# Weight lo parts and one convolution tile of the second block: summed by adding DMA transfers instead of VectorE and GpSimd

## The chip, the cores and the metric

The kernel runs on one core of a Trainium2 chip. Its time is what the device takes for one launch, in microseconds (us); the times shown are the median and the extremes of three runs, and one more execution was recorded by the hardware profiler. The engines are TensorE (PE; its weight loads are PEld), VectorE (DVE), ScalarE (ACT), GpSimd (POOL) and SyncE (SP), which issues the ordinary DMA transfers. Each engine works through its own list of instructions in order.

## The reference, cut to what matters

Two transformer blocks follow each other on a sequence of 1024 tokens of width 1024, all in float32. The first has a Fourier mix, a latent attention, a cross attention to a memory and a mixture of 16 experts. The second is the one that the change touches:

```python
h = rmsnorm(x) * (1 + scale) + shift
proj = h @ w_in                       # 1024 x 10240
glu_a, glu_b, z_conv, q, k, v, z_att, g_conv, g_att = split(proj)
u = glu_a * sigmoid(glu_b)
u = depthwise_conv(u, conv_w, 31 taps, causal) + conv_b
y_conv = (silu(layernorm(u)) * silu(z_conv)) @ w_conv_out
y_att  = dilated window attention of q, k, v in three groups, times silu(z_att), @ w_att_out
x = x + gate * ((sigmoid(g_conv) * y_conv + sigmoid(g_att) * y_att) @ w_o)
```

## The kernel before, in words

**Split numbers.** TensorE multiplies in a short format (float32r), so every operand is split into a hi part (the value rounded to that format) and a lo part (value less hi), and a product is made of three matmuls: hi hi, hi lo, lo hi (`mm3`, `gemm_t`, lines 676 to 688). `split_to` (line 653) makes the hi part with a copy on ScalarE, and the lo part with a subtraction on VectorE or GpSimd; `ve()` (line 645) deals these calls out in a fixed ratio, in the second block one in four to GpSimd, at its end one in eight.

**Weight tiles.** `in2` (line 1597) makes one 128-channel tile of `proj`: it loads a 128 x 8 x 128 weight tile (512 KB) on SP, splits it (`wtile`, line 665) and runs 48 matmuls of 512 columns on it. There are 80 such tiles. In each group of three matmuls the last needs the lo part of the weights.

**Convolution.** `conv_tile` (line 1619) makes the gated input `u` of 128 channels, and then 31 taps of a shifted multiply and add into a page `o` (`conv`). Seven of the eight tiles do it on VectorE, one instruction for each tap. Tile 3 (`POOL_CONV`) does it in two: ScalarE multiplies a shifted `u` into a page `ct`, and GpSimd adds it to `o`. The taps are not issued at once: `tick` (line 690) takes one or two off a list after each half of a weight tile's matmuls, and ties them to these matmuls.

**Attention.** `att_pair` (line 1697) runs 12 times: q, k and v tiles by `in2`, the rotary positions on VectorE (`rope2`: `rt`, `rq`, `ro`), stacked copies on ScalarE (`qs`, `ks`), zeros on GpSimd (`kl`), ScalarE's copy of v (`vf`), its transposes on TensorE (`vt`), then scores, softmax and the product with v. Tiles of gates (`z_conv`, `z_att`, `g_att`, later `g_conv`) lie between as filling.

**Planner.** All operations of the program are recorded first, with a price and a latency, and `schedule` (line 283) orders them by a list rule: of the operations that are ready on an engine, the one recorded earliest. It lays buffers into 50 equal SBUF pages (`PAGES`, 4 KB on each of 128 partitions). An operation that needs a new page may start early only while the count of pages that all operations before it still need leaves one over; if not, it is held until earlier operations are done (`allowed`, line 310). What follows an operation waits for its end, which includes its latency, plus 0.5 us on another engine; on the same engine the latency is taken off again (line 378):

```python
lat = op.end + (self.LAT if o.eng != e else (0.07 if e == "dve" else 0.0) - op.lat)
```

The order that comes out is fixed in the program; at run time each engine keeps it and waits for the true ends. The profile puts nearly all instructions on one line, L180, the recording helper, so they are told apart by their tiles' names.

Of the kernel before, what the change touches and what calls it, by code (L numbers as in the profile page):

```python
# [8 lines left out]
F32 = mybir.dt.float32  # L9
F32R = mybir.dt.float32r  # L10
# [3 lines left out]
ACT = mybir.ActivationFunctionType  # L14
AX = mybir.AxisListType
P = 128
NT = 1024
# [171 lines left out]
class Program:  # L189
# [199 lines left out]
    def issue(self, order):  # L389
        with self.tc.manual_schedule():  # L390
            for op in order:
                for t in op.new:
                    pool, tag = self.pools[t.kind]
                    t.real = pool.tile(list(t.shape), t.dt, tag=f"{tag}{t.slot}", name=t.name)
                op.fn()
# [135 lines left out]
IN2 = {"glu_a": 0, "glu_b": 8, "z_conv": 16, "q": 24, "k": 36, "v": 48, "z_att": 60, "g_conv": 64, "g_att": 72}  # L531
# [47 lines left out]
class Kern(Program):  # L579
# [819 lines left out]
    def scatter_add(self, rows, idx, x):  # L1399
# [3 lines left out]
                in_=x.ap(), in_offset=None, compute_op=OP.add)  # L1403
        self.record("pool", 1.3, 4.0, issue, [x, idx], [rows]).dma = 1.46

    def tr8(self, x, base, n=8):

        h, l = self.page(base + "h", F32R, (P, 8, P)), self.page(base + "l", F32R, (P, 8, P))
        for c in range(0, n, 4):
            m = min(4, n - c)  # L1410
            ps = self.pb(base, (P, m, P))
            for k in range(m):
                self.pe.transpose(ps[:, k], x[:, (c + k) * P:(c + k + 1) * P], self.ident)
            self.split_to(h[:, c:c + m], l[:, c:c + m], ps, lo="dve")
        return h, l
# [180 lines left out]

    def in2(self, part, m, evac):
        n = len(self.ops)
        w = self.wtile(self.a["w_in2"][IN2[part] + m], 8, "w2")
        if self.in2_free:  # L1600
            self.in2_free -= 1
        else:
            self.ops[n].deps.add(self.x3_loaded)
        self.ops[n + 1].deps.add(self.moe_end)
        self.gemm_t(w, self.h2, evac, base=part, ticks=TICKS[part[0]])
# [13 lines left out]
    def conv_tile(self, i, cd):  # L1619

        u = self.in2_tanh("glu_b", i, "u")
        self.in2("glu_a", i, lambda c, ps: self.dve.scalar_tensor_tensor(u[:, c], u[:, c], 1.0, ps, OP.add, OP.mult))
        o = self.page("conv")
        w = lambda t: self.convw[:, i, t:t + 1]
        b = GV2["conv_b"] + i
        if i in POOL_CONV:
            back = self.back[1].append
            back(lambda: self.act.activation(o, u, ACT.Identity, scale=w(30), bias=self.gv2[:, b:b + 1]))

            def mul(t, n):  # L1630
                self.conv_tmp = self.page("ct")
                return self.act.activation(self.conv_tmp[:, :n], u[:, :n], ACT.Copy, scale=w(t))

            for t in range(29, -1, -1):
                s = 30 - t
                back(lambda t=t, s=s: mul(t, NT - s))
                back(lambda s=s: self.pool.tensor_tensor(o[:, s:], o[:, s:], self.conv_tmp[:, :NT - s], OP.add))
        else:
            back = self.back[0].append
            tap = self.dve.scalar_tensor_tensor  # L1640
            back(lambda: self.dve.tensor_scalar(o, u, w(30), self.gv2[:, b:b + 1], OP.mult, OP.add))
            for t in range(29, -1, -1):
                back(lambda t=t, s=30 - t: tap(o[:, s:], u[:, :NT - s], w(t), o[:, s:], OP.mult, OP.add))
        back(lambda: self.sp.dma_start(cd[i], o))
        back(lambda: self.conv_add(o))
# [383 lines left out]
```

## Time and profile before

| | us |
|---|---|
| median of 3 runs | 2770.51 (2767.68 to 2771.46) |
| the profiled execution, its own time | 2771.41 |
| its span, first to last instruction | 2769.3 |
| TensorE busy | 2659.9 |
| VectorE busy | 2096.2 |
| ScalarE busy | 1362.1 |
| GpSimd busy | 505.6 |

The span is what the traced instructions cover; busy time is the union of an engine's instructions in it. The second block's weight tiles begin at 1467 us and end at 2541 us. The granted clock is TensorE's: 1.00 is the upper of its two levels (2.4 GHz), 0.50 the lower (1.2 GHz).

### The profile page before, as it was taken

The page shows a single profiled execution, that of the slowest core. Times are in us where ns is not written, and L with a number is a line of the kernel's source. Part 1 is how long each engine was busy: PE and PEld are TensorE (multiplying, and loading weights), DVE is VectorE, ACT ScalarE, POOL GpSimd, SP SyncE. Part 2 cuts the span into 40 slices and gives each one's busy share as a digit, 9 for nine tenths or more (in the row PEclk, how much of TensorE's full clock was granted, in tenths as well). Part 3 has the DMA queues.
Part 4 walks back from the last instruction along what each step waited for, and adds up shares of the span by engine and source line. Part 5 has one row for each costly group of instructions (what it writes and reads, how often), then busy time and mean ns, then how long its engine had stood idle before and what let it go on. Part 6 is the DMA issues. An engine that isn't in the chain of part 4 may idle for free. (4 is left out here: it accounts for less than half of the span.)

```text
span 2769.3 us, 36068 instructions
## 1 busy us (share of the span) xinstructions
PE 2659.9 (96%) x13230; PEld 2232.0 (81%) x13230; DVE 2096.2 (76%) x3075; ACT 1362.1 (49%) x2177; POOL 505.6 (18%) x270
## 2 busy tenths in 40 slices
PE   8999999999994999999988998999999999999998
PEld 6888888888884888888867877788888888887887
DVE  7367876457567989988978789988889997649553
ACT  6156776333345877777774154534334434524221
POOL 1025555211004200101110133401100002002000
PEclk9999999999996999999999999999999999999999
DMA  4100112545347999999984011212212233449941
GB/s 174 34 34 9 39 54 92 175 154 180 124 139 283 342 358 359 357 356 387 380 302 172 16 61 61 77 54 90 78 42 73 77 137 138 152 164 309 340 173 53
DMA packets 130144, 457.06 MB, mean 165 GB/s; under 512 B 15299, under 2 KB 17539, under 8 KB 129969
## 3 DMA queue, kind: packets, MB, share of 16 engines
q1 hardware_dynamic: 125360, 438.00, 43.7%
q0 software_dynamic: 4608, 16.78, 2.4%
q8 instruction: 104, 1.70, 0.2%
q14 instruction: 72, 0.58, 0.1%
HBM read 378.73 MB, written 69.70 MB: 162 GB/s over the span
## 5 line engine op out<-in xcount | busy, mean ns | idle before, releaser
L180 DVE SCALAR_TENSOR_TENSOR conv<-u,convw,conv 128x1003 f32<-128x1003 f32 (+19 forms) x210 | 298.0, 1426 | 2.2
L180 DVE TENSOR_TENSOR w_upl<-w_up,w_uph 128x1024 fp32r<-128x1024 f32 x128 | 149.2, 1221 | 22.6 <-ACT w_uph L180 21.7
L180 DVE TENSOR_TENSOR w_downl<-w_down,w_downh 128x1024 fp32r<-128x1024 f32 x128 | 149.0, 1222 | 13.3 <-ACT w_downh L180 12.5
L180 DVE TENSOR_TENSOR w_gatel<-w_gate,w_gateh 128x1024 fp32r<-128x1024 f32 x123 | 144.0, 1220 | 7.5 <-ACT w_gateh L180 5.2
L180 ACT CAST w_gateh<-w_gate 128x1024 fp32r<-128x1024 f32 x128 | 125.7, 1057 | 5.7 <-issue 3.3
L180 ACT CAST w2h<-w 128x1024 fp32r<-128x1024 f32 x80 | 83.2, 1050 | 88.9 <-DMA w<-in_w_in_dram 62.1
L180 ACT CAST w_downh<-w_down 128x1024 fp32r<-128x1024 f32 x128 | 126.0, 1054 | 1.4 <-PE ea L180 1.4
L180 ACT CAST w_uph<-w_up 128x1024 fp32r<-128x1024 f32 x128 | 125.7, 1055 | 1.4 <-PE ea L180 0.7
L180 DVE TENSOR_TENSOR w2l<-w,w2h 128x1024 fp32r<-128x1024 f32 x64 | 87.2, 1364 | 37.7 <-ACT w2h L180 19.8
L180 POOL TENSOR_TENSOR wl<-w,wh 128x1024 fp32r<-128x1024 f32 (+3 forms) x31 | 57.3, 1849 | 310.6 <-ACT wh L180 253.3
L180 ACT CAST wh<-w 128x1024 fp32r<-128x1024 f32 (+3 forms) x71 | 62.5, 894 | 78.4 <-DMA w<-in_w_convout_dram 31.6
L180 ACT ACTIVATE ap<-ap,amx 128x128 f32<-128x128 f32 (+1 forms) x192 | 85.5, 449 | 25.5 <-DVE amx L180 25.2
L180 POOL TENSOR_TENSOR conv<-conv,ct 128x1023 f32<-128x1023 f32 (+29 forms) x30 | 74.8, 2493 | 115.5 <-ACT ct L180 115.1
L180 POOL TENSOR_TENSOR w2l<-w,w2h 128x1024 fp32r<-128x1024 f32 x16 | 43.8, 2734 | 263.2 <-ACT w2h L180 208.4
L180 DVE TENSOR_TENSOR ptl<-pt,pth 128x512 fp32r<-128x512 f32 x128 | 81.4, 684 | 8.7 <-ACT pth L180 6.7
L180 ACT ACTIVATE p<-p,mx 128x1024 f32<-128x1024 f32 x64 | 73.8, 1155 | 23.6 <-DVE mx L180 17.3
L180 POOL TENSOR_SCALAR p<-p,sum 128x1024 f32<-128x1024 f32 x64 | 74.2, 1166 | 59.0 <-DVE sum L180 52.7
L180 PE MATMUL eb<-w_uph,hth 128*128 128x512 f32 x256 | 80.5, 394 | 0.1
L1401 POOL DMA_INDIRECT x<-ey,idx x16 | 25.4, 1586 | 302.4 <-ACT ey L180 193.7
L180 PE MATMUL eb<-w_upl,hth 128*128 128x512 f32 x256 | 79.6, 392 | 0.7 <-DVE w_upl L180 0.5
L180 PE MATMUL ea<-w_gateh,hth 128*128 128x512 f32 x256 | 80.1, 393 | 0.0
L180 PE MATMUL ea<-w_gatel,hth 128*128 128x512 f32 x256 | 79.6, 392 | 0.4 <-DVE w_gatel L180 0.4
(554 smaller groups left out, 8663.1 us busy)
## 6 DMA issues: line engine op xcount, KB each, us to landing
w_gate<-in_w_gate_dram SPq DMA_DIRECT2D x128, 512.0 KB, 6.7
w_up<-in_w_up_dram SPq DMA_DIRECT2D x128, 512.0 KB, 6.9
w_down<-in_w_down_dram SPq DMA_DIRECT2D x128, 512.0 KB, 8.1
w<-in_w_in_dram SPq DMA_DIRECT2D x89, 512.0 KB, 4.1
wada<-in_w_adaT_dram SPq DMA_DIRECT2D x24, 512.0 KB, 6.4
convr<-cd SPq DMA_DIRECT2D x16, 512.0 KB, 6.2
amd<-sg SPq DMA_DIRECT2D x16, 512.0 KB, 5.7
ks<-ks SPq DMA_DIRECT2D x24, 256.0 KB, 2.9
```

The lines of the kernel that those rows point to most:

```text
L180: getattr(k.engines[eng], fn)(*[r(x) for x in a], **{n: r(x) for n, x in kw.items()})
L1401: self.nc.gpsimd.indirect_dma_start(out=rows.ap(), out_offset=bass.IndirectOffsetOnAxis(ap=idx.ap(), axis=0), in_=x.ap(), in_offset=None, ...
```

## The change

In `in2` the lo part is no longer a subtraction. ScalarE makes the hi part as before, and then a second copy, the negated hi part, into the lo part's page. A DMA transfer issued by GpSimd adds the raw weights to that page (`add_dma`, a new helper). In `conv_tile`, for tile 3, the addition of each tap to `o` is such a transfer as well, in place of GpSimd's tensor addition; ScalarE's multiplications stay. The planner is told a price of 1.1 us on GpSimd, a latency of 3.0 us, and the transfer's share of SP's queue.

```diff
+    def add_dma(self, out, x):
+
+        def issue():
+            self.nc.gpsimd.dma_start(out=out.ap(), in_=x.ap(), accum_op=OP.add)
+        op = self.record("pool", 1.1, 3.0, issue, [x, out], [out])
+        op.dma = 4 * int(np.prod(x.shape)) / 360e3
+        return op
...
     def in2(self, part, m, evac):
         n = len(self.ops)
-        w = self.wtile(self.a["w_in2"][IN2[part] + m], 8, "w2")
+        raw = self.load(self.a["w_in2"][IN2[part] + m], "w2", (P, 8, P), "wr")
+        w = [self.page("w2" + q, F32R, (P, 8, P)) for q in "hl"]
+        self.act.copy(w[0], raw)
+        self.act.activation(w[1], w[0].bitcast(F32), ACT.Copy, scale=-1.0)
+        self.add_dma(w[1].bitcast(F32), raw)
...
                 s = 30 - t
                 back(lambda t=t, s=s: mul(t, NT - s))
-                back(lambda s=s: self.pool.tensor_tensor(o[:, s:], o[:, s:], self.conv_tmp[:, :NT - s], OP.add))
+                back(lambda s=s: self.add_dma(o[:, s:], self.conv_tmp[:, :NT - s]))
```

## Rows read from the trace of the kernel before

**Rows 1.** The page, part 1: busy us, share of the span, instructions of TensorE.
```profile
PE 2659.9 (96%) x13230; PEld 2232.0 (81%) x13230; DVE 2096.2 (76%) x3075; ACT 1362.1 (49%) x2177; POOL 505.6 (18%) x270
```

**Rows 2.** Stretches: us; busy (count) of PE, PEld, DVE, ACT, POOL; clock; DMA; GB/s.
```profile
1445.00:1467.00 22.00, 8.41 (x44) 6.33 (x42) 11.21 (x22) 12.23 (x21) 3.19 (x2) 0.70 0.83 286
1467.00:2541.00 1074.00, 1042.66 (x5120) 875.10 (x5121) 899.15 (x1348) 427.54 (x869) 162.03 (x67) 0.98 0.29 99
1567.00:1800.00 233.00, 214.67 (x1039) 179.13 (x1038) 205.08 (x286) 112.02 (x214) 90.56 (x40) 0.96 0.18 59
2446.00:2541.00 95.00, 89.91 (x390) 74.00 (x388) 79.82 (x55) 29.69 (x42) 13.54 (x2) 0.96 0.74 235
```

**Rows 3.** Waits of TensorE, 1440 to 2560 us: total, times, longest.
```profile
PE vt L180 <- ACT vf L180: 13.4, 5, 7.2
```

**Rows 4.** Order of time on TensorE: start, length, instruction, idle before and releaser.
```profile
1671.11 1.76 PE L180 MATMUL vt<-ident,vf 128*128 128x128 f32 x7 [7.21 <-ACT vf L180]
...
1740.31 1.86 PE L180 MATMUL vt<-ident,vf 128*128 128x128 f32 x8 [3.49 <-ACT vf L180]
```

**Rows 5.** Stretches as in rows 2, around these two waits.
```profile
1668.80:1679.00 10.20, 7.09 (x31) 6.70 (x32) 8.08 (x25) 7.97 (x19) 0.00 (x0) 0.50 0.22 51
1740.40:1744.00 3.60, 3.60 (x15) 3.21 (x15) 3.57 (x2) 1.65 (x3) 3.16 (x2) 0.53 0.43 101
```

**Rows 6.** The page, part 5: groups of instructions; busy us, mean ns, idle before.
```profile
L180 ACT CAST w2h<-w 128x1024 fp32r<-128x1024 f32 x80 | 83.2, 1050 | 88.9 <-DMA w<-in_w_in_dram 62.1
...
L180 DVE TENSOR_TENSOR w2l<-w,w2h 128x1024 fp32r<-128x1024 f32 x64 | 87.2, 1364 | 37.7 <-ACT w2h L180 19.8
...
L180 POOL TENSOR_TENSOR conv<-conv,ct 128x1023 f32<-128x1023 f32 (+29 forms) x30 | 74.8, 2493 | 115.5 <-ACT ct L180 115.1
L180 POOL TENSOR_TENSOR w2l<-w,w2h 128x1024 fp32r<-128x1024 f32 x16 | 43.8, 2734 | 263.2 <-ACT w2h L180 208.4
```

**Rows 7.** Groups on VectorE, 1567 to 1800 us, columns as in rows 6.
```profile
L180 DVE SCALAR_TENSOR_TENSOR conv<-u,convw,conv 128x1002 f32<-128x1002 f32 (+29 forms) x44 | 82.2, 1868 | 0.5
L180 DVE TENSOR_TENSOR w2l<-w,w2h 128x1024 fp32r<-128x1024 f32 x12 | 19.4, 1614 | 6.0 <-DMA od<-of 2.2 <-DMA cd<-conv 1.9 <-PE apt L180 1.7
```

**Rows 8.** The same for 1800 to 2446 us.
```profile
L180 DVE SCALAR_TENSOR_TENSOR conv<-u,convw,conv 128x1019 f32<-128x1019 f32 (+21 forms) x146 | 190.0, 1311 | 1.3
```

**Rows 9.** Line 1401, the experts' adding scatter (512 KB): ns min/median/max; landing.
```profile
L1401 POOL DMA_INDIRECT x<-ey,idx x16: 1552/1588/1612, 933.3 to 1444.1; - x16
...
DMA to landing us min/median/max: 6.4/9.9/11.1
```

**Rows 10.** DMA: queue with packets, MB, share of 16 engines; issues with median landing.
```profile
q0 software_dynamic: 4608, 16.78, 2.4%
...
od<-of SPq DMA_DIRECT2D x12, 512.0 KB, 2.6
```

**Rows 11.** Order of time, several engines: weight tiles split at the last moment.
```profile
1470.95 1.04 ACT L180 CAST w2h<-w 128x1024 fp32r<-128x1024 f32 x1
1511.59 1.22 DVE L180 TENSOR_TENSOR w2l<-w,w2h 128x1024 fp32r<-128x1024 f32 x1 [2.39 <-PE glu_b L180]
1514.11 0.39 PE L180 MATMUL glu_a<-h2h,w2l 128*128 128x512 f32 x1
...
2074.29 2.40 POOL L180 TENSOR_TENSOR w2l<-w,w2h 128x1024 fp32r<-128x1024 f32 x1 [92.12 <-ACT w2h L180]
2077.83 0.49 PE L180 MATMUL z_att<-h2h,w2l 128*128 128x512 f32 x1 [0.61 <-DVE w2l L180]
...
2518.48 1.06 ACT L180 CAST w2h<-w 128x1024 fp32r<-128x1024 f32 x1 [6.18 <-DMA w<-in_w_in_dram]
2528.09 0.80 PE L180 MATMUL g_conv<-h2h,w2l 128*128 128x512 f32 x1 [5.09 <-DVE w2l L180]
```

**Rows 12.** A tile split early: its subtraction; its matmuls (ns; first, last start).
```profile
1529.44 1.22 DVE L180 TENSOR_TENSOR w2l<-w,w2h 128x1024 fp32r<-128x1024 f32 x1
...
L180 PE MATMUL k<-h2h,w2l x192: 389/389/398, 1576.9 to 2392.0; 128*128 128x512 f32 x192
```

## The prediction

> **What bounds the kernel now.** I read the busy shares first: TensorE is busy for 96% of the span [rows 1], so a change that touches no matmul can only win or lose the gaps between matmuls. Then the stretches: from 1467 to 2541 us lies all of the work that the diff touches (80 weight tiles, the convolution, the attention), and of these 1074 us TensorE is busy 1042.66, so 31.3 us are gaps; ScalarE is busy 427.5 and has room [rows 2]. The gaps are not even: 18.3 us of them lie between 1567 and 1800 us, where VectorE is busy 88% and GpSimd does its share of the convolution, and 5.1 us after 2446 us [rows 2]. The waits of TensorE say what ends them: 13.4 us are transposes of v that wait for ScalarE's copy [rows 3], 5.1 us is one wait for the lo part of a weight tile [rows 11]. Two of the waits for v make 10.7 us of the 13.4 [rows 4], and they cost twice: around them the granted clock is at 0.50 and 0.53, the lower level, for 10.2 and 3.6 us [rows 5]. ScalarE is late there because its copy of v stands behind the copy of k, which waits for VectorE's rotary sum, and VectorE is full.
>
> **What the change does to each engine.** ScalarE gets 80 negated copies; a copy of that size takes 83.2/80 = 1.04 us [rows 6], so 83 us more in 1074, 40% becoming 48%. I cost that at nothing, except where a tile is late anyway (below), since ScalarE was busy under half of the time; without that cover each copy would put its 1.04 us ahead of an exponential or a copy that TensorE waits for. VectorE loses 64 subtractions, 87.2 us, and GpSimd 16 subtractions and 30 additions, 43.8 + 74.8 us [rows 6]. GpSimd gets 110 transfers to issue in their place.
>
> **The gain: VectorE between 1567 and 1800 us.** Twelve subtractions leave this stretch, 19.4 us [rows 7]. More goes with GpSimd's additions: a tap on VectorE takes 1868 ns here [rows 7] and 1311 ns once GpSimd's taps are over [rows 8]. Without GpSimd's tensor operations I take the shorter value: 44 x 0.557 = 24.5 us, so some 44 us of 205 in all. The waits for v go with it: 7.21 + 3.49 us [rows 4], and half of the 7.09 and 3.60 us that TensorE worked at the low level [rows 5], 5.3 us. That is 16 us; I take 14, because the copy of k stays ahead of that of v on ScalarE. The bounds are 0 (the waits move to another producer) and 20 (all 18.3 us of gaps there and some clock). After 1800 us VectorE's relief buys next to nothing: there TensorE hardly waits [rows 2].
>
> **The price: how long a summed transfer takes.** No row shows a transfer that adds into SBUF. The nearest is the scatter that adds into DRAM, the same 512 KB from the same queue: 1.55 us or more to issue, and 6.4 us (least), 9.9 (median), 11.1 (most) to landing, in a stretch with full DMA engines [rows 9]. From below, a plain 512 KB store from SBUF lands after 2.6 us [rows 10]. I take 6.4: it is an adding transfer, and between 1467 and 2446 us the DMA engines are mostly free. For most tiles even 9.9 us are hidden, because the lo part was ready 7 to 57 us before its first matmul (the tile of the first k is subtracted at 1529.44 us and used at 1576.9 [rows 12]; one row of 73 such). It is not hidden for seven tiles of 80, whose lo part is made at the last moment: the first is subtracted at 1511.59 us and used at 1514.11, and one on GpSimd at 2074.29 is used at 2077.83; the last is copied at 2518.48 and used at 2528.09 [rows 11]. In the first the hi part had been ready since 1472 us, and VectorE itself stood idle for 2.39 us before the subtraction [rows 11]; so it was no lack of speed. What holds such a tile is the SBUF page: the planner lets an operation that needs a new one start only when the 50 pages allow it, and I assume that this point doesn't move with the change. From there the path was one subtraction (1.22 us, or 2.40 on GpSimd [rows 11]); it becomes 1.04 us of copy plus 6.4 us, 7.45 us. Tile by tile, the start of the old subtraction plus 7.45 less the old first use gives 4.9 us for the first and 3.9 us for the one at 2074 [rows 11]; from the same pairs of rows 3.9, 5.4 and 3.8 us for three others between 1600 and 1760 us. For the one at 1769 us I take 3, because its transfer is queued on GpSimd behind two taps, the second of which now waits for the landing of the first. The last has its copy ready at 2519.5 us, stands behind an addition on GpSimd, and the DMA engines are 74% busy [rows 2]: between no loss (6.4 us) and 7 us (9.9 us behind that addition), I take 3. The sum is 27.9 us. TensorE can fill some of it with hi products of other chains, two per chain before each needs its lo part; I take a fifth off, 23 us. Each new gap of that length also brings some 3.6 us at the low level [rows 5], which gives away 1.8 us; two of the seven places have that already and one pays little, so four are new, 7 us. The price is 30 us; with 2.6 us to landing it would be 4, with 9.9 us 55.
>
> **What stands in which queue.** The transfer to be summed waits on GpSimd for the negated copy, and the 24 memsets of the key pages and the transfers of later tiles stand behind it. The taps are the worse case: each adds to the page that the one before it writes, so it waits for that landing. The planner doesn't see this: for a follower on the same engine it takes the latency off again, and puts the taps 1.1 us apart. At 6.4 us thirty taps take 192 us, and they now spread over 229 us, paced by TensorE; so they fit, with a lag of a few us in the dense parts, and nothing reads the result before 2300 us. I cost the lag at nothing beyond the 3 us above, because a normal tile has 7 us or more to spare. Loads on SP: the new transfers share the DMA engines. One transfer of the software queue takes 2.4% of 2769.3 us over 32 transfers, 2.1 us of all sixteen engines [rows 10]; 110 of them are 229 us, in a stretch where the engines are some 29% busy over 1074 us [rows 2], so there is room for them. At the start there is less: three tiles are split while the block's input is being loaded, 22 us at 83% [rows 2]; 3 x 2.1 = 6.2 us meet 3.7 us of room, so the input and TensorE come 2.5 us later (between 0 and 6.2). The calls that were alternated between VectorE and GpSimd are now dealt out differently after the weight tiles drop out; one such operation takes 2.7 us on GpSimd and 1.36 on VectorE [rows 6], so it is bound by a few of these differences on either side, and I take 0.
>
> **The sum** is made against the profiled execution, 2771.41 us (its span is 2769.3, 2 us less; the median of the runs is 0.9 us below it): 2771.4 - 14 + 30 + 2.5 = 2789.9, and against the median 2789. A GpSimd that issues faster than the scatter (no index list) makes me round to 2788.
>
> **Rivals.** First, faster: the summed transfer lands like a plain one. With 2.6 us [rows 10] the price is 4 us, the start costs 1, the gain of 14 stays: 2771 - 14 + 5 = 2762, and 2757 if the gain is 20 and the start free. For it: SBUF to SBUF spares DRAM. Against it: every adding row is at 6.4 us or more [rows 9]. The point from which it decides is a landing of some 4 us. The Trainium skill (DMA: Bandwidth & Descriptors, "Anatomy of one DMA — SWDGE (gpsimd) path") prices a transfer from GpSimd at 2.0 us plus its bytes over 436 GB/s, which is an estimate of 3.2 us for 512 KB and so this rival; the scatter's 6.4 us disagree with it, in a busier stretch. Second, much slower: the taps become the bound. At the scatter's median of 9.9 us [rows 9] thirty taps need 297 us where TensorE leaves 233 [rows 2]; GpSimd runs in order, so the weight tiles' transfers stand behind the taps and TensorE follows the difference, 64 us, beside the 55: 2771 + 64 + 55 - 14 = 2876 at the full price, and 2830 if half of it is covered by the tiles' lead. For it: a chain with a landing in each link. The Trainium skill (DMA: Bandwidth & Descriptors, "Rules for kernel authors") says that an adding transfer may meet no other access to its bytes before its landing has been signalled, which is what makes the chain; no run here has shown it. Against it: between 1567 and 1800 us the DMA engines are 18% busy [rows 2]. Third, no change: the held tiles find other matmuls to cover them and the price sinks to the gain, 2771 +- 5.
>
> **How the numbers follow.** The forecast has 0.52, the faster rival 0.25, the taps 0.13, no change 0.10. The range goes from 2752 (the faster rival with some luck in the order of the plan) to 2832 (the taps half covered); the forecast's own is 2772 to 2805. A measurement of this kernel tells about 0.2%, 5.5 us, from no change. Slower by more: nearly all of the 0.52, the 0.13, and little else, 0.63. Within: 0.12, from the third rival and the edges of the others. Faster by more: 0.25.
>
> **What would show it.** Right: waits of TensorE for the lo part's landing, five to seven of 2 to 6 us, at tiles made late; none of 7 us for v between 1567 and 1800 us; a tap on VectorE at 1.3 us throughout; summed transfers that land 5 to 8 us after issue. Wrong: landings under 4 us (then the first rival), taps on GpSimd issued one landing apart without pause and waits for the lo part at most tiles (the second), or a plan in which the late tiles are not late.

## The result, and the profile after

The changed kernel takes 2793.82 us (median of 4 runs, 2789.90 to 2798.70), the kernel before on the same chip 2770.99 (2767.68 to 2771.84). The ratio is 1.0083, with a 95% interval of 1.007 to 1.0096: 23 us slower, by 19 to 27. The forecast was 2788, slower. The profiled execution of the changed kernel took 2796.02 us, with a span of 2794.2; it is one of the longer ones, so differences between single traces come out 2 us larger than those of the medians.

The busy shares, answering to [rows 1]: VectorE has lost 131 us, ScalarE has gained 79, and TensorE is still at 96%.

```profile
PE 2668.8 (96%) x13230; PEld 2235.2 (80%) x13230; DVE 1964.8 (70%) x3014; ACT 1441.0 (52%) x2257; POOL 466.7 (17%) x331
```

The stretches, columns as in [rows 2]. Between 1567 and 1800 us VectorE went from 205 to 145 us, and the DMA engines from 18% to 62%. TensorE did not gain from it: 213.54 us of work in that stretch, where it did 214.67. In the first stretch the DMA engines are busier than before and move less (231 GB/s, before 286). The last two lines, the first of the kernel before and the second of the changed one, hold the same matmuls, from the first product of the fourth q tile to that of the first `g_conv` tile: this middle part is 6.7 us shorter than before.

```profile
1445.00:1467.00 22.00, 8.04 (x32) 5.84 (x30) 5.38 (x12) 12.11 (x18) 3.31 (x4) 0.61 0.91 231
1567.00:1800.00 233.00, 213.54 (x1016) 175.97 (x1015) 145.05 (x272) 119.71 (x222) 39.31 (x45) 0.95 0.62 141
...
1803.72:2446.10 642.38, 637.39 (x3252) 538.90 (x3250) 529.71 (x905) 257.15 (x574) 50.02 (x21) 0.99 0.28 96
...
1822.28:2457.97 635.69, 634.23 (x3252) 536.00 (x3250) 475.47 (x866) 304.61 (x623) 59.98 (x60) 1.00 0.51 140
```

The waits of TensorE from 1440 to 2600 us (total, times, longest). Three kinds end with the landing of a summed transfer: 13.0 us before the last tile, 4.9 before the fourth, 2.6 before the twenty-first. The wait for the block's input has grown to 12.8 us from 8.0 (start of TensorE's work on it at 1456.85 us, before at 1454.39, and a second wait of 2.3), and the block's first product comes 5.55 us later, as the first two lines below show, the upper of the kernel before. The waits for v are 8.8 where they were 13.4 [rows 3]: one of 7.1 is left.

```profile
1467.19 0.80 PE L180 MATMUL glu_b<-h2h,w2h 128*128 128x512 f32 x1 [1.58 <-ACT h2h L180]
...
1472.74 0.79 PE L180 MATMUL glu_b<-h2h,w2h 128*128 128x512 f32 x1 [1.58 <-ACT h2h L180]
...
PE g_conv L180 <- DMA w2l<-w: 13.0, 1, 13.0
PE h L180 <- DMA x<-x: 12.8, 2, 10.5
PE vt L180 <- ACT vf L180: 8.8, 3, 7.1
PE glu_a L180 <- DMA w2l<-w: 4.9, 1, 4.9
...
PE glu_b L180 <- DMA w2l<-w: 2.6, 1, 2.6
```

The line that issues the adding transfers (ns least/median/most, first and last start; landing in us): 0.86 us on GpSimd for one, and 5.0 us to landing in the middle case, 4.5 at the least. It answers to [rows 9]. The queue of [rows 10] went from 2.4% of the span to this share:

```profile
L1409 POOL DMA_DIRECT2D w2l<-w x80: 852/859/1246, 1449.3 to 2542.0; - x80
L1409 POOL DMA_DIRECT2D conv<-ct x30: 859/859/1210, 1582.6 to 1822.0; - x30
...
DMA to landing us min/median/max: 4.5/5.0/11.6
```

```profile
q0 software_dynamic: 20448, 74.22, 13.5%
```

13.5% of 2794.2 us less 2.4% of 2769.3 is 311 us of all sixteen engines for 110 transfers, 2.8 us each; the forecast took 2.1.

The fourth tile, in order of time. Its negated copy is made at 1513.55 us, although its hi part was there at 1477.55; that is 2 us after the old subtraction [rows 11]. By the planner's rule it is the point at which a page comes free; the trace shows the order, and not the page. The transfer is issued at 1515.22 and used at 1524.37, after 9.2 us, in a stretch in which the DMA engines are full; three transfers for later tiles follow in 7 us.

```profile
1513.55 1.05 ACT L180 ACTIVATE w2l<-w2h 128x1024 fp32r<-128x1024 f32 x1
...
1515.22 0.87 POOL L1409 DMA_DIRECT2D w2l<-w  x1
...
1524.37 0.80 PE L180 MATMUL glu_a<-h2h,w2l 128*128 128x512 f32 x1 [4.88 <-DMA w2l<-w]
```

The last tile. Its load is issued late (2525.63), its copies are done at 2536.5, and the transfer then stands on GpSimd behind an addition of 8.02 us that belongs to the attention. TensorE waits 13.01 us, before 5.09 [rows 11].

```profile
2525.63 0.34 SPq L180 DMA_DIRECT2D w<-in_w_in_dram  x1
...
2534.07 8.02 POOL L180 TENSOR_TENSOR at<-at,at 128x1024 f32<-128x1024 f32 x1 [32.47 <-DVE at L180]
2534.37 1.04 ACT L180 CAST w2h<-w 128x1024 fp32r<-128x1024 f32 x1 [4.96 <-DMA w<-in_w_in_dram]
2535.44 1.06 ACT L180 ACTIVATE w2l<-w2h 128x1024 fp32r<-128x1024 f32 x1
...
2542.05 0.86 POOL L1409 DMA_DIRECT2D w2l<-w  x1
2549.21 0.80 PE L180 MATMUL g_conv<-h2h,w2l 128*128 128x512 f32 x1 [13.01 <-DMA w2l<-w]
```

Around these two waits the clock is at its lower level, as it is around those of [rows 5]; the columns are those of the stretches:

```profile
1523.70:1530.50 6.80, 6.13 (x14) 4.84 (x15) 0.00 (x0) 2.10 (x2) 0.86 (x1) 0.50 1.06 242
...
2537.40:2554.50 17.10, 5.29 (x13) 4.13 (x14) 14.87 (x13) 7.38 (x7) 5.50 (x2) 0.50 0.99 326
```

The wait of 7.1 us for v. ScalarE stands still for 7.90 us before its copy, and what ends that is no product of TensorE or VectorE but the landing of a tap's transfer, issued at 1742.82:

```profile
1742.82 0.86 POOL L1409 DMA_DIRECT2D conv<-ct  x1 [4.15 <-issue]
...
1747.46 0.58 ACT L180 COPY vf<-v 128x512 f32<-128x512 f32 x1 [7.90 <-DMA conv<-ct]
...
1749.61 1.97 PE L180 MATMUL vt<-ident,vf 128*128 128x128 f32 x8 [7.13 <-ACT vf L180]
```

The copy of v does not read what the taps write. It waits because its page held a product of a tap. Of the waits for taps' transfers from 1567 to 1830 us those of GpSimd are the chain itself; the others are of that kind:

```profile
POOL conv L1409 <- DMA conv<-ct: 23.1, 6, 7.0
ACT vf L180 <- DMA conv<-ct: 7.9, 1, 7.9
...
DVE rq L180 <- DMA conv<-ct: 5.0, 1, 5.0
...
DVE ro L180 <- DMA conv<-ct: 3.7, 1, 3.7
```

And the taps on VectorE in 1567 to 1800 us, answering to [rows 7], 1868 ns each there:

```profile
L180 DVE SCALAR_TENSOR_TENSOR conv<-u,convw,conv 128x1004 f32<-128x1004 f32 (+29 forms) x41 | 51.7, 1261 | 0.4
```

### The profile page after: what moved, and what is told of

Read it like the earlier page. It is cut to its first block, busy times and chain, and to the rows that moved or that the text cites. A ratio compares the mean times of both kernels' runs of the same rounds, so it can differ in the third digit from the quotient of the medians.

```text
span 2794.2 us, 36360 instructions
## 1 busy us (share of the span) xinstructions
PE 2668.8 (96%) x13230; PEld 2235.2 (80%) x13230; DVE 1964.8 (70%) x3014; ACT 1441.0 (52%) x2257; POOL 466.7 (17%) x331
## 3 DMA queue, kind: packets, MB, share of 16 engines
q0 software_dynamic: 20448, 74.22, 13.5%
## 5 line engine op out<-in xcount | busy, mean ns | idle before, releaser
L180 DVE SCALAR_TENSOR_TENSOR conv<-u,convw,conv 128x995 f32<-128x995 f32 (+20 forms) x210 | 264.7, 1265 | 2.7
L1409 POOL DMA_DIRECT2D w2l<-w x80 | 70.0, 875 | 651.2 <-ACT w2l L180 447.6
L180 ACT ACTIVATE w2l<-w2h 128x1024 fp32r<-128x1024 f32 x80 | 84.8, 1060 | 26.8 <-DMA w2l<-w 9.0
L180 ACT ACTIVATE ap<-ap,amx 128x128 f32<-128x128 f32 (+1 forms) x192 | 85.3, 450 | 22.3 <-DVE amx L180 20.7
L180 PE MATMUL ey<-w_downh,gtl 128*128 128x512 f32 x256 | 79.0, 390 | 0.9 <-DVE gtl L180 0.9
L180 PE MATMUL ey<-w_downh,gth 128*128 128x512 f32 x256 | 79.5, 391 | 0.1
```

Of the source, the lines that this page charges most:

```text
L180: getattr(k.engines[eng], fn)(*[r(x) for x in a], **{n: r(x) for n, x in kw.items()})
L1409: self.nc.gpsimd.dma_start(out=out.ap(), in_=x.ap(), accum_op=OP.add)
```

## The experiments

Theory A was that the loss is made where tiles are late: three at the start, those held for a page, and the last; and that the relief of VectorE gains a little through the waits for v. The rivals were that it is spread over all transfers as contention, that ScalarE's further copies make it, or that the chain of taps does. In the table the ratio is to the kernel before on the same chip, and the last column is that ratio, less 1, times 2771 us.

| kernel | ratio, 95% interval | us against before |
|---|---|---|
| the changed kernel | 1.0083 (1.007 to 1.0096) | +23.0 |
| e1, taps alone by transfers | 0.998 (0.997 to 0.9989) | -5.5 |
| e2, weights alone by transfers | 1.0084 (1.0067 to 1.0101) | +23.3 |
| e3, seven late tiles subtracted | 1.0008 (0.9999 to 1.0018) | +2.2 |
| e4, planner told of the landing | 1.0141 (1.0124 to 1.0158) | +39.1 |
| e5, first three tiles subtracted | 1.0063 (1.0046 to 1.0079) | +17.5 |
| e6, three held tiles subtracted | 1.0046 (1.0029 to 1.0063) | +12.7 |
| e7, sums made by engines | 1.0033 (1.0022 to 1.0043) | +9.1 |
| e8, last seven tiles subtracted | 1.0065 (1.0048 to 1.0082) | +18.0 |
| e9, two sums of taps | 1.0132 (1.0117 to 1.0148) | +36.6 |
| e10, taps alone, two sums | 1.0075 (1.0061 to 1.0089) | +20.8 |
| e11, transfers in the middle only | 0.9976 (0.9967 to 0.9985) | -6.7 |
| e12, pages kept for the products | 1.0083 (1.0069 to 1.0097) | +23.0 |

The traces divide these differences further. Between the points below each of these kernels runs the same number of matmuls; the points are the first product on a weight tile, and the numbers are the us from one to the next in one trace each. The first row differs by up to 2 us also between kernels that do nearly the same there (before, e1, e11).

| from, to | before | changed | e1 | e2 | e7 | e11 |
|---|---|---|---|---|---|---|
| start, first weight tile | 1467.2 | 1472.7 | 1467.6 | 1471.7 | 1468.6 | 1465.4 |
| first weight tile, first q tile | 98.4 | 106.3 | 98.3 | 105.1 | 97.6 | 98.5 |
| first q tile, fourth q tile | 238.2 | 243.3 | 231.7 | 243.2 | 241.1 | 231.4 |
| fourth q tile, first `g_conv` tile | 642.4 | 635.7 | 642.5 | 636.0 | 642.5 | 637.7 |
| first `g_conv` tile, last | 76.3 | 77.5 | 76.3 | 77.9 | 76.3 | 76.3 |
| last `g_conv` tile, end | 246.9 | 258.8 | 247.8 | 254.5 | 255.2 | 252.9 |

**One half of the change at a time.** e1 takes the weights back, e2 the taps:

```diff
 e1, in in2
-        raw = self.load(self.a["w_in2"][IN2[part] + m], "w2", (P, 8, P), "wr")
...
-        self.add_dma(w[1].bitcast(F32), raw)
+        w = self.wtile(self.a["w_in2"][IN2[part] + m], 8, "w2")
 e2, in conv_tile
-                back(lambda s=s: self.add_dma(o[:, s:], self.conv_tmp[:, :NT - s]))
+                back(lambda s=s: self.pool.tensor_tensor(o[:, s:], o[:, s:], self.conv_tmp[:, :NT - s], OP.add))
```

> Only the taps of tile 3 are summed by transfers; the weight tiles' lo parts are subtractions as before. Theory A (the loss is the weight tiles': the transfer's 5 us to landing where the lo part is made at the last moment, and the block's start): none of it is left, and GpSimd's tensor additions, which lengthen VectorE's taps, are gone: 2757 to 2768 us. Theory B (the loss is the chain of taps: each waits for a landing, the planner sets them 1.1 us apart and gives their pages on too early, so that ScalarE and VectorE wait for landings): slower than before, 2775 to 2785 us, with a wait of TensorE for v of 7 us between 1700 and 1760 us.

> Only the weight tiles' lo parts are summed by transfers; the taps of tile 3 are added by GpSimd as before. Theory A: nearly all of the loss stays, 2785 to 2800 us, with the waits of TensorE for w2l at the fourth tile (5 us) and at the last (some 10 us). Theory B: the loss goes, 2765 to 2775 us.

e1 took 2765.15 us and e2 2792.56. The weights make the whole loss; the taps alone are a gain of 5.5 us. TensorE's waits in e1, from 1440 to 2600 us, show what is gained and what is given back: those for v are down from 13.4 to 1.7 us, and two kinds have come up; the longest of each stands behind an operation of VectorE that waited for a tap's landing.

```profile
PE ao L180 <- DVE aptl L180: 4.5, 2, 3.8
...
PE as L180 <- DMA ks<-ks: 2.6, 2, 2.1
...
PE vt L180 <- ACT vf L180: 1.7, 3, 1.0
```

```profile
1725.07 2.02 DVE L180 TENSOR_TENSOR ro<-rq,rt 128x1024 f32<-128x1024 f32 x1 [3.68 <-DMA conv<-ct]
...
1750.57 1.29 DVE L180 TENSOR_TENSOR aptl<-apt,apth 128x512 fp32r<-128x512 f32 x2 [3.37 <-DMA conv<-ct]
```

e2 keeps the waits for the input (12.5), the fourth tile (4.7) and the last (11.0), and has those for v in full (13.2). The two halves would be +17.8 together, -5.5 and +23.3, and the whole is +23.0; the 5.2 us between them are no more than the uncertainty. The stretches do show it: from the first to the fourth q tile e1 takes 6.4 us less than the kernel before, and e2 and the changed kernel both take 5 us more. Beside the weights' transfers the taps' gain is gone.

**The late tiles, together and one place at a time.** Four kernels make the lo part of some tiles on VectorE again and leave all else as it is in the changed kernel:

```diff
     def in2(self, part, m, evac):
+        self.in2_n = getattr(self, "in2_n", -1) + 1
+        if self.in2_n in (0, 1, 2, 3, 12, 20, 79):     # e3
+        if self.in2_n in (0, 1, 2):                    # e5
+        if self.in2_n in (3, 12, 20):                  # e6
+        if self.in2_n >= 73:                           # e8
+            w = self.wtile(self.a["w_in2"][IN2[part] + m], 8, "w2", lo="dve")
+        else:
...
```

> The changed kernel, but seven of the 80 weight tiles (the first four, the 13th, the 21st and the last) get their lo part by VectorE's subtraction again. Theory A: the start comes 5 us earlier, the waits for w2l at the fourth, the 21st and the last tile go (4.9 + 2.6 + 13.0 us, of which 5 us at the last were there before), and their low clock: 20 to 25 us back, 2768 to 2775 us. Theory B: only the tiles' own waits go and the wait for v stays; 2780 to 2788 us.

> The changed kernel, but the weights of the first three input tiles of the second block are subtracted on VectorE as before, so that no adding transfer runs beside the eight loads of the norm's input. A (the start is one of the places where the loss arises: the adding transfers lengthen those loads): the first product of the block starts about 5 us earlier again, and what is left does not depend on it, 2786 to 2790 us. B (rival: the start is later because of what came before, or the gain is eaten by the waits that follow): within 2 us of the changed kernel, 2792 to 2796.

> The changed kernel, but three tiles that are loaded late (the fourth, the thirteenth and the twenty-first of the input weights) are subtracted on VectorE. A (a tile whose load is late pays for the longer way to its lo part): the waits of 4.9 and 2.6 us before the fourth and the twenty-first go, with 3.4 to 5 us that the clock's fall behind them costs, 2781 to 2787. B (rival: the loss is spread evenly over all transfers, as contention of the DMA engines with the other loads): 3 tiles of 80 give back 1 us at most, 2792 to 2795.

> The changed kernel, but the last seven tiles of the input weights are subtracted on VectorE. A (the last tile, whose load is late, pays for the longer way): the wait of 13.0 us before its first use falls to some 5 us, and with it 3 us of low clock, 2781 to 2787. B (rival: the load of the last tile is late in the changed kernel for another reason, the pages it needs, and stays late whatever makes its lo part): a wait of 8 us or more is left and the time is 2788 to 2793.

Seven tiles of 80 make 20.8 of the 23 us (e3, 2772.75 us). Alone, the start gives back 5.5 (e5, 2789.50 us), the three held tiles 10.2 (e6, 2784.58 us; their three subtractions are 4% of the tiles), and the last seven 5.0 (e8, 2789.20 us): 20.7 in all, which agrees with e3, although each difference is known only to some 4 to 6 us, so that the start and the last tile alone are hardly clear of it. Contention spread over all transfers would have given 2 us for e3. The waits answer one by one. In e5 the input's is 7.7 us, as before the change, the block's first product comes at 1466.77 us, and the waits for the tiles stay, 4.9, 4.6 and 12.3 us:

```profile
PE h L180 <- DMA x<-x: 7.7, 1, 7.7
PE glu_a L180 <- DMA w2l<-w: 4.9, 1, 4.9
```

In e6 the two waits of `glu_a` and `glu_b` for a landing are gone but for 0.4 us and the others stay (input 12.8, last tile 10.9). In e8 the last tile's is 5.9 us and ends with VectorE:

```profile
PE g_conv L180 <- DVE w2l L180: 5.9, 1, 5.9
```

That is A on the wait; in time, 2789.20 us, e8 is where B had it, and part of what the last tile gave back went to a wait of 2.3 us for a split of the last stage, 0.5 in the changed kernel.

**Transfers where tiles are early.** e11 has the same edit with the condition turned round: transfers for tiles 24 to 72 only, the other 31 subtracted on VectorE; the taps are transfers.

```diff
+        if not (24 <= self.in2_n <= 72):
+            w = self.wtile(self.a["w_in2"][IN2[part] + m], 8, "w2", lo="dve")
+        else:
...
```

> The changed kernel, but only the 49 input tiles from the twenty-fifth to the seventy-third, most of which are loaded 15 us or more ahead of their use, get their lo part by a transfer; the other 31 are subtracted on VectorE, the taps stay transfers. A (a transfer costs only where the tile is loaded late, and relieving VectorE in a stretch where TensorE is busy 99% gains nothing): the time with the taps alone, ratio 0.997 to 0.9995. B (rival: the cost is spread over all 80, 28 us in all by the difference of the changed kernel and the taps alone): 49 of 80 make 17 us, ratio 1.003 to 1.006. C (rival: the relief pays in the middle too): ratio under 0.9965.

2765.69 us, a ratio whose interval overlaps with that of e1: A on the time, where 49 of the 80 transfers cost nothing. That the relief gains nothing where TensorE is nearly always busy is not what the stretches show. From the fourth q tile to the first `g_conv` tile VectorE has 480 us of work in e11 where e1 has 527 (530 before the change), and the same matmuls take 4.7 us less than in e1:

```profile
1795.19:2432.92 637.73, 634.50 (x3252) 535.96 (x3250) 479.53 (x869) 304.01 (x622) 57.67 (x58) 1.00 0.50 137
```

All kernels with transfers in this part are shorter in it than the kernel before, by 1 us (e4) to 7 us, and those that subtract there (e1, e7, e10) are not; whether that is VectorE's relief itself or the order that comes with it was not separated. e11 gives it back from the last tile on, 5.2 us against e1, of which 2.8 are a longer wait for a split of the last stage (3.3 us).

e11 and e1 are the fastest kernels here, 0.2% under the kernel before; their times can't be told apart.

**The copy without the transfer.** e7 keeps ScalarE's second copy of every tile, and lets VectorE and GpSimd add.

```diff
-        self.add_dma(w[1].bitcast(F32), raw)
+        self.ve().tensor_tensor(w[1], raw, w[1].bitcast(F32), OP.add)
```

> The changed kernel with ScalarE's second, negated copy of every weight tile kept, but the sum of the copy and the raw tile is made by VectorE and GpSimd (64 and 16 tiles, the mix of the kernel before) and not by a transfer. The taps stay transfers. A (the loss comes from the transfer: its issue, its landing, its packets): 2763 to 2772, the time with the taps alone or a few us more. B (rival: the loss comes from ScalarE's 80 further copies of 1 us in the way of its other work, and from one more step in the chain): 2782 or more.

2780.59 us is neither: 14.7 us above e1 and 13.9 below the changed kernel. So the extra step on ScalarE, which I had costed at nothing for tiles that aren't late, goes with about half of the weights' 28.5 us. Where it costs can be seen only in part, in TensorE's waits of e7: 7.7 us are a late tile again, which now waits for ScalarE's first copy.

```profile
PE glu_a L180 <- ACT w2h L180: 7.7, 1, 7.7
```

```profile
PE fo L180 <- ACT mgh L180: 4.9, 1, 4.9
PE ya L180 <- ACT wh L180: 3.4, 3, 1.5
PE ya L180 <- DVE wl L180: 1.2, 1, 1.2
```

The second fence is the same view from 2541 to 2770 us, after the last weight tile, in a stage that the edit doesn't touch; the kernel before waits 0.2 us there. No copy of a weight tile is left in it, so these 9.5 us go, as far as the trace tells, with the order that the planner made of the whole. The stretches narrow the rest: 48 of the 80 copies lie between the fourth q tile and the first `g_conv` tile, where e7 takes 642.5 us as e1 does, so copies are not dear everywhere. Nearly all of the difference lies between the first and the fourth q tile (9.4 us, with the wait of 7.7 in it) and from the last tile on (7.5). How much of that is the copies themselves stays open.

**The taps' chain.** Four kernels went at the landings of the taps, three of them at the wait of 7.1 us for v. e4 tells the planner what a transfer takes, and that a follower on the same engine waits for it too:

```diff
 where the planner is set up
+        self.landing = set()
 in schedule
-                lat = op.end + (self.LAT if o.eng != e else (0.07 if e == "dve" else 0.0) - op.lat)
+                lat = op.end + (self.LAT if o.eng != e or op.i in self.landing else (0.07 if e == "dve" else 0.0) - op.lat)
 in add_dma
-        op = self.record("pool", 1.1, 3.0, issue, [x, out], [out])
+        op = self.record("pool", 0.9, 4.1, issue, [x, out], [out])
+        self.landing.add(op.i)
```

> The changed kernel, but the planner is told what the trace shows of a summed transfer (0.9 us to issue, 4.1 us more to landing) and lets an instruction that follows one on GpSimd wait for the landing. Theory B: taps are planned a landing apart and their pages given on in time, so the wait for v of 7.1 us goes with its low clock: 2780 to 2787 us. Theory A: the late tiles stay late, 2790 to 2798 us.

2808.88 us: both expectations fell. The order is another, and its waits are worse. The longest new one, of 6.8 us, is for ScalarE's exponential; ScalarE stands still for 6.50 us before a tap's product, whose page is read by a transfer not yet landed, and the exponential is queued behind:

```profile
1635.00 1.14 ACT L180 ACTIVATE ct<-u,convw 128x1016 f32<-128x1016 f32 x1 [6.50 <-DMA conv<-ct]
...
1637.30 2.66 PE L180 MATMUL apt<-ident,ap 128*128 128x128 f32 x10 [6.79 <-ACT ap L180]
```

e9 (on the changed kernel) and e10 (on e1) add the taps in turn into two pages:

```diff
+            o2 = self.page("conv2")
             back(lambda: self.act.activation(o, u, ACT.Identity, scale=w(30), bias=self.gv2[:, b:b + 1]))
+            back(lambda: self.pool.memset(o2[:, :1], 0.0))
+            back(lambda: self.act.activation(o2[:, 1:], u[:, :NT - 1], ACT.Copy, scale=w(29)))
...
-            for t in range(29, -1, -1):
-                s = 30 - t
+            for t in range(28, -1, -1):
+                s, acc = 30 - t, (o, o2)[t % 2]
                 back(lambda t=t, s=s: mul(t, NT - s))
-                back(lambda s=s: self.add_dma(o[:, s:], self.conv_tmp[:, :NT - s]))
+                back(lambda s=s, acc=acc: self.add_dma(acc[:, s:], self.conv_tmp[:, :NT - s]))
+            back(lambda: self.pool.tensor_tensor(o, o, o2, OP.add))
```

> The changed kernel, but the 29 transfers of the convolution tile add in turn into two pages, which GpSimd adds up at the end, so that a transfer need not wait for the landing of the one just before it. A (the wait of 7.1 us before the transposition of v comes from ScalarE standing still until a page comes free whose transfer is queued behind the landings of others): the taps get through faster, that wait falls under 3 us, 2784 to 2790 us. B (rival: that wait is the price of ScalarE's own work, 112 us before and 120 after in the stage, whatever the taps do): the wait stays at 6 to 8 us, 2791 to 2797.

> The kernel with the taps alone as transfers (weights subtracted as before), with the two sums. A (the waits of 2.1 and 3.8 us that came up in it at 1731 and 1751 come from the same queue of landings): 2 to 6 us less than with one sum, ratio to the kernel before 0.996 to 0.9975. B (rival: there VectorE is the late one, and the queue of the taps costs nothing): within 1.5 us of one sum, ratio 0.9975 to 0.999.

2807.97 and 2790.91 us, 14 and 26 us more than with one sum: all four expectations missed. The chain itself did ease: in e10 GpSimd waited for landings 4 times and 20.7 us in all where e1 has 15 and 67.7. The waits on pages became longer. This is e10's longest one on TensorE, 11.9 us for the copy of k, and two waits of VectorE before it:

```profile
1704.91 0.69 DVE L180 SCALAR_TENSOR_TENSOR rq<-q,cos 128x512 f32<-128x512 f32 x1 [7.36 <-DMA conv<-ct]
...
1732.46 1.87 DVE L180 TENSOR_TENSOR ro<-rq,rt 128x1024 f32<-128x1024 f32 x1 [4.67 <-DMA conv<-ct]
...
1738.54 0.44 PE L180 MATMUL as<-ks,qs 128*128 128x128 f32 x1 [11.88 <-DMA ks<-ks]
```

The second sum also holds a page of the 50 for the whole tile; whether that or the new order makes the rest was not separated. So the fault was looked for in the pages, and e12 keeps two of them for the products alone:

```diff
+            cts = [self.page("ct") for _ in range(2)]
 in mul
-                self.conv_tmp = self.page("ct")
+                self.conv_tmp = cts[t % 2]
```

> The changed kernel, but the products of the taps go in turn into two pages that are kept for them over the whole tile, so that no other value is written into a page that a transfer not yet landed still reads. A (the wait of 7.1 us before the transposition of v at 1750 us, and VectorE's waits of 5.0 and 3.7 us for q and k, come from pages of the products that the planner hands on before the transfer has landed): no instruction but the products themselves and the transfers waits for a tap's transfer, the wait before v falls under 3 us, and 2783 to 2789 us, a ratio of 1.0045 to 1.0068 to the kernel before. B (rival: ScalarE, which now makes the products in two pages only, stands still for the landing in the products themselves and holds up the copies of v just the same): the wait stays at 5 us or more, 2790 to 2797 us, ratio 1.007 to 1.0098.

On the waits A held: of VectorE's work and of the copies of v none waits for a tap any more (one copy of a weight tile does, for 2.1 us), and TensorE's wait for v is 1.1 us at most (from 1567 to 1830 us, below). On the time A fell: 2791.89 us, the ratio of the changed kernel and within what B had. What B named came too: ScalarE now stands still for 36.3 us before ten of its products, where the changed kernel has 2.6. On TensorE the place of the wait for v was taken by waits for the weights' lo parts, 9.5 us in four rows where the changed kernel has 2.6 in that stretch, and by one for k:

```profile
ACT ct L180 <- DMA conv<-ct: 36.3, 10, 9.4
...
PE glu_b L180 <- DMA w2l<-w: 3.9, 1, 3.9
PE as L180 <- DMA ks<-ks: 2.9, 2, 2.7
PE z_conv L180 <- DMA w2l<-w: 2.2, 1, 2.2
PE q L180 <- DMA w2l<-w: 1.8, 1, 1.8
PE vt L180 <- ACT vf L180: 1.6, 2, 1.1
PE glu_a L180 <- DMA w2l<-w: 1.6, 1, 1.6
```

So the page that is handed on too soon is shown as the cause of the 7.1 us, and it is shown as well that taking it away in this way is worth nothing. Whether ScalarE's new waits or the new order brought the others was not separated.

## Why the prediction was right, and where it was not

The direction and the place were right: the loss is made at late tiles, and 2793.82 us is inside the range and inside the forecast's own. The sum came within 6 us by luck: two terms were off in opposite directions, the price by 15 us and the gain by 14. Of the signs named for it, the tap at 1.3 us came, and the landings were a little shorter than the 5 to 8 us named; three waits for a landing came and not five to seven, and one wait of 7 us for v stayed.

**The landing** was taken at 6.4 us, between 2.6 and 9.9; it was 5.0, with 4.5 as the least, above the 4 us from which the faster rival would have decided. The estimate of 3.2 us from the Trainium skill (DMA: Bandwidth & Descriptors, "Anatomy of one DMA — SWDGE (gpsimd) path") does not agree with these landings; no transfer of the 110 came under 4.5 us, and the measurement decides. The second rival did not come true: the taps spread over 239 us (1582.6 to 1822.0 us), paced by the stage as expected.

**The price, 30 us,** was twice what was found: 10.2 for the held tiles and 5.0 for the last, by e6 and e8. The mechanism fits the one described, a lo part that can be begun at much the same point whoever makes it and is then longer on its way; that the page sets this point is the planner's rule, and no run tested it. For the first of the seven even the size was right, 4.9 us forecast and 4.88 measured, by an accident: the landing was longer (9.1 us) and the first matmul later. But only three of the seven made TensorE wait for a landing. For the tile at 2074 us, costed at 3.9, the prediction took the wrong row: the matmul at 2077.83 waits for VectorE, as its line says [rows 11], whose subtraction ran from 2074.77 to 2077.77 us and would give 4.4; the sum on GpSimd at 2074.29 belongs to a q tile that is used at 2093.43. The tile used at 2077.83 is no longer held in the new order, where its lo part has landed 49 us ahead; a tile's lateness belongs to one plan, and the change made another. The last tile was undersized the other way: 7.9 us more of waiting, forecast 3, because its load came 16 us later, where TensorE came to it only 13 later, and the addition ahead of it on GpSimd took 8.02 us.

**The start, 2.5 us,** was 5.5, near the upper bound of 6.2 (e5). A summed transfer takes 2.8 us of all engines on average and not 2.1, and the engines were 91% busy in the stretch. The first product, 5.55 us later in the changed kernel and back at 1466.77 us in e5, says the same as the times.

**The gain, 14 us,** is the step that failed. VectorE's relief came as forecast, and more (60 us in the stretch, forecast 44; the tap at 1261 ns). But the step "the waits for v go with it" took VectorE as what holds up ScalarE's copy of v. With the taps alone as transfers the gain is 5.5 us; with the weights too it is none (e2 against the changed kernel). The lag of the taps was costed at nothing, since nobody reads their sum before 2300 us. That looked at the reader of the sum only. The product pages have readers as well, the transfers; the planner takes a page as free after its own price, and whoever is given it waits for a landing (7.90 us for the copy of v, 5.0 and 3.7 for VectorE). The prediction had noted that the planner does not see the landing and did not follow that to the pages. Where it put the relief at next to nothing, after 1800 us, the middle part is 6.7 us shorter; in the changed kernel that offsets the 5.1 us which the part from the first to the fourth q tile lost.

**ScalarE's copies** were costed at nothing except in late tiles. e7 puts the copies and the order that they bring at 14.7 us of the weights' 28.5; that is more than nothing, although the 48 copies of the middle part cost nothing there; how the rest divides is open.

With the measured terms the sum is 0 + 10.2 + 5.0 + 5.5 = 20.7 of the 23.0 us. The remaining 2.3 are within the uncertainty.

Three figures of the prediction are off by its own terms, and none decides anything: a fifth off 27.9 is 22.3 and not 23; the faster rival at its best is 2771 - 20 + 4 = 2755 and not 2757; and the slower rival's 2830 leaves out the gain of 14 that its 2876 counts, with which half the loss gives 2816.

## What to carry to other kernels

Moving an operation to a slower route costs only where its result is wanted at once: sort the places by how long the result lies before its first use, and change only those with time to spare (49 of 80 here, at no cost). Where the bound engine hardly waits, relief of another engine buys little (at most 7 us of 642 here, and e11 lost it again further on): the most that such a change can reach is the few waits it ends and the low clock around them. Compare kernels between the same matmuls, and not between the same times, or such a part is not seen. And when a scheduled operation gets a landing that the scheduler underrates, ask who gets the buffers that it reads, not only who reads its result.

## What the runs showed of the hardware that was not expected

An adding transfer of 512 KB within SBUF took 4.5 us at the least to land, and 9.1 to 11.6 where the DMA engines were full (4 issued within 7 us). Another transfer was slower beside them: the attention's store of 512 KB from SBUF, 2.6 us to landing in [rows 10] and 2.8 in e1, took 4.6 in the changed kernel and 4.9 in e2. A tap on VectorE, 1868 ns beside GpSimd's additions and subtractions [rows 7], took 1264 in e1, where GpSimd no longer adds the taps, and 1622 in e2, where it still does but subtracts no weights. And the addition on GpSimd ahead of the last tile's transfer, 3.33 us in the kernel before, took 8.02 in the changed one and 8.20 in e8. Such lengths are not new with the change: in the kernel before the GpSimd subtraction just ahead of that addition, of the same size, took 10.25 us. The profile calls GpSimd's spans rough, and no run here looked for the cause.
